# Ten parts of the output projection, one job or ten, in the table that orders TensorE's instructions

## The chip, the cores and the metric

One core of one Trainium2 chip. The metric is the device time of one execution of the kernel in microseconds (us); smaller is better. Three runs of the kernel before gave 1026.78, 1026.9 and 1029.99 us, median 1026.9.

## The reference

A trunk of four decoder layers over 512 tokens of width 1024, everything in float32. Each layer projects its input, runs attention with 16 heads of 64 value columns, multiplies the heads' outputs by a SiLU gate, projects back, adds the result to the scaled input and normalizes. The attention differs by layer: latent attention (layers 0 and 3), a sliding window of 128 with sinks (layer 1), a softmax with a forget-gate bias (layer 2).

```python
for i in range(DEPTH):                       # 4 layers
    kind = i % 3                             # mla, swa, fox, mla
    h = x @ w_in                             # q, k, v (or their low ranks) and the gate
    o = attention(h)                         # 16 heads x 64, 512 x 1024
    y = (o * jax.nn.silu(gate)) @ w_out      # the output projection: contraction over 1024
    x = layernorm(alpha * x + y) * ln_g[i] + ln_b[i]
```

## The kernel before

**Numbers in halves.** TensorE works here on fp32r values. Each operand is kept as a high part and a low rest, and each product is made of three matmuls: high by high, low by high, high by low. So a projection of one output tile of 128 tokens by 512 columns over 1024 rows takes 8 blocks of 128 rows, 3 matmuls each.

**A layer.** `run_heads` (L654) issues the middle of a layer: the projections that are still missing (K, Q, R, V and gate G, as generators that issue one matmul at a time and then yield), and for each head three kinds of attention steps. The s steps are logits: matmuls into a PSUM tile `ss` for each block of 128 queries; VectorE adds the bias or mask and finds the maximum (L885, L947, L1067, L1069), and after the last block `softmax_tail` (L445) has ScalarE make the exponentials, VectorE the reciprocal `rs`, and GpSimd and ScalarE the scaling of the P tiles. The t steps transpose P on TensorE into a PSUM tile `ptt`; `pt_evac` (L497) copies it to `PT` as high (ScalarE, L500) and low (VectorE, L325). The o steps multiply PT with V into the single PSUM tile `oo`; at the end of a head ScalarE copies one half (L543) and VectorE adds the other (L544), which frees `oo`. After the second head of a pair, the pair's output is multiplied by its gate (L551, GpSimd, or VectorE for the last pair) and becomes a block of `oT`: high by a ScalarE cast (L552), low by a subtraction (L325, on GpSimd or VectorE). Block k of `oT` is head pair k. Two blocks share one tile, so `oT` of blocks 4 and 5 has one name.

**The output projection.** An output tile is (half, tb): half 0 or 1 of the 1024 columns, tb one of four blocks of 128 tokens. `out_mm` (L570) issues its matmuls for a list of blocks ks, three per block: k's weight block `w` (or `wo`) against `oT` block k. Each output tile accumulates in a PSUM tile of its own; those of half 0, tb 0 to 2 come from the pool of three banks `pp`, which the projections use as well. `out_part` (L557) makes ten parts, in this order: (0,0), (0,1), (0,2) each over blocks 0 to 5, the same three over block 6, then (1,0), (1,1), (1,2), (0,3) over blocks 0 to 6. Block 7 comes after the attention, in `finish` (L705).

**TensorE's order.** The order of TensorE's instructions is not left to the scheduler. `ORDER` (above `layer_units`) holds one string of words for each layer; a word is a letter and a count. s, t and o take so many steps from the logits, the transposes and the P·V products of the heads in turn. f, g and h take so many steps from the first, second and third job of a list `jobs` (f = `jobs[0]`, g = `jobs[1]`, h = `jobs[2]`). A job is `[steps left, generator]`; when `jobs[0]` has no steps left it is dropped and the others move up. The projections of `STREAM` are a job each, and behind them stands one job of nominally 1000 steps, which is the whole of `out_part`. A g or h that points past the end of the list takes the last job (`min(..., len(jobs) - 1)`). So once only the output projection is left, f, g and h all mean the same: its next matmul. The last words of three layers:

```python
# layer 1: ... s2 f1 s2 f19 s2 g1 s2 g14 o3 t4 o5 f1 t3 g1 f7 o8
# layer 2: ... f6 t3 f3 g14 o1 g1 s2 t3 o3 f1 g1 s2 h6 t4 h2 s2 h1 f2 o1 f1 o3 f1 s2 t3 f3 t3 o8
# layer 3: ... f5 o4 f7 t4 f1 g4 o1 f1 s6 f6 o3 t3 f4 t3 f2 o8
```

`tail` (L692) and `finish` (L705) take what is left of the output projection from `st["order"]`, in counts of their own, around the last two heads. The other engines execute in the order that the scheduler gives them; each waits for TensorE and for each other through semaphores.

Of the kernel before, what the change touches and what calls it, by code (L numbers as in the profile page):

```python
# [200 lines left out]
class Net:  # L201
# [355 lines left out]
    def out_part(self, layer, st):  # L557

        st["acc"] = {}
        st["done"] = 0  # L560
        st["stat"] = self.p_st.tile([128, NT, 4], F32, tag="stat", name=self.nm("stat"))
        self.load_residual(layer, st)
        parts = [(0, tb, range(6)) for tb in range(3)] + [(0, tb, [6]) for tb in range(3)]
        parts += [(half, tb, range(7)) for half, tb in ((1, 0), (1, 1), (1, 2), (0, 3))]
        for half, tb, ks in parts:
            for _ in self.out_mm(layer, st, half, tb, list(ks), False):
                st["done"] += 1 if self.fine else 3
                yield

    def out_mm(self, layer, st, half, tb, ks, stop):  # L570
        if (half, tb) not in st["acc"]:
            if (half, tb) in ((1, 0), (1, 1)):
                st["acc"][(half, tb)] = self.ps_s.tile([128, 512], F32, tag="ss", name=self.nm("po"))
            elif (half, tb) in ((1, 2), (0, 3)):
                st["acc"][(half, tb)] = self.ps_t.tile([128, 512], F32, tag="pt", name=self.nm("po"))
            else:
                st["acc"][(half, tb)] = self.bank()
        out = st["acc"][(half, tb)][:]
        oT = st["oT"]
        return self.tokproj_steps(out, lambda k: (self.W(layer, "O", half, k // 2), (k % 2) * 512), 512,  # L580
                                  lambda k, a, b: oT[k // 2][:, k % 2, a, b * 128:(b + 1) * 128], tb, ks, ks[0] == 0, stop, 3)
# [72 lines left out]
    def run_heads(self, layer, st, make, pre=None, npre=0):  # L654

        kind = layer % 3
        st["P"], st["PT"], st["oT"] = {}, {}, []
        st["np"] = 3 if kind == 0 else 2
        self.heads = 0

        def size(n):
            return {"K": 6, "Q": 9, "R": 9}.get(n, 24) if kind == 0 else 96 if n == "V" else 24

        def logits():
            for h in range(H - 1):
                if h == 13 and kind == 0:
                    self.cq_done(layer)
                for i, f in enumerate(st["s_fn"](h, st)):
                    for j, _ in enumerate(f()):
                        if i == NT - 1 and j == st["np"] - 1:  # L670
                            self.head_done()
                        yield

        jobs = [[npre, pre]] if npre else []
        jobs += [[size(n), make[n](a)] for n, a in STREAM[kind]]
        st["order"] = self.out_part(layer, st)
        jobs.append([1000, st["order"]])
        runs = {"s": logits(), "t": chain.from_iterable(f() for h in range(H - 2) for f in st["t_fn"](h, st)),
                "o": chain.from_iterable(self.attn_pv(h, st) for h in range(H - 2))}
        self.fine = True  # L680
        with self.tc.manual_schedule(engines={mybir.EngineType.PE}):
            for w in ORDER[layer].split():
                for _ in range(int(w[1:])):
                    job = jobs[min("fgh".index(w[0]), len(jobs) - 1)] if w[0] in "fgh" else [0, runs[w[0]]]
                    next(job[1])
                    job[0] -= 1
                    while jobs[0][0] == 0:
                        jobs.pop(0)
            assert len(jobs) == 1 and all(next(r, None) is None for r in runs.values())
            self.tail(layer, st)  # L690

    def tail(self, layer, st):  # L692
# [448 lines left out]
```

## Time and profile before

| | before |
|---|---|
| median of three runs | 1026.9 us |
| the profiled execution's own time | 1026.01 us |
| its span, first to last instruction | 1024.2 us |
| mean granted TensorE clock | 0.986 |
| ScalarE, VectorE, GpSimd busy | 620.8, 598.3, 510.7 us |
| DMA | 116.79 MB, 114 GB/s in the mean |

Layer 1 ends near 470 us, layer 2 near 770 us. Engines are named PE (TensorE matmul), PEld (its weight load), ACT (ScalarE), DVE (VectorE), POOL (GpSimd), SP (DMA issue). A row of a timeline holds the start, the time from the first start to the last end, the engine, line, operation, tiles, form and count; in brackets the idle time before it and what ended that. Durations of neighbouring matmuls overlap, since they are pipelined: the pace is read from start to start. A row of the windows view holds the stretch, its length, PE's busy time and instructions, the granted clock, and the DMA's share and GB/s.

### The profile page before, as it was taken

Reading aid. Unit: us, or ns where it says so; the run is one execution under the profiler, and the core shown is the slowest. Engines: PE = TensorE matmul, PEld = TensorE weight load, DVE = VectorE, ACT = ScalarE, POOL = GpSimd, SP = SyncE. Lnnn points to the kernel's source line nnn. Section 1 sums busy time; section 2 is a strip of 40 time slices with the busy share of each in tenths; the row PEclk is TensorE's granted clock in tenths of the full one; section 3 lists DMA queues with packets and bytes.
Section 4 is the critical chain, followed back from the end, with each engine's and each line's share of the span. In section 5 each row is a group of like instructions: output and inputs, shape, how many; then the busy total and the mean of one; then the engine's idle time right before and its main releaser. Section 6 shows DMA issues by size and latency. Waiting matters only on the chain.

```text
span 1024.2 us, 16213 instructions
## 1 busy us (share of the span) xinstructions
PE 985.8 (96%) x5512; PEld 856.9 (84%) x5512; DVE 598.3 (58%) x1501; ACT 620.8 (61%) x1354; POOL 510.7 (50%) x572
## 2 busy tenths in 40 slices
PE   8999999999999999899999999997999999999995
PEld 7979888877988888688888888985779888888784
DVE  2467666935546667528325644664547466667827
ACT  4378888843357777523446766663533478888722
POOL 5746655335156663432556666543254647664213
PEclk9999999999999999899999999998999999999998
DMA  6353332634342213223434323353224354334322
GB/s 225 119 157 92 98 106 66 205 111 146 133 143 84 83 63 124 91 94 128 133 120 141 105 88 120 91 144 120 84 84 146 97 145 127 85 94 124 103 62 83
DMA packets 37795, 116.79 MB, mean 114 GB/s; under 512 B 5440, under 2 KB 5696, under 8 KB 37456
## 3 DMA queue, kind: packets, MB, share of 16 engines
q1 hardware_dynamic: 37712, 115.75, 36.5%
q8 instruction: 44, 0.72, 0.3%
q14 instruction: 39, 0.32, 0.1%
HBM read 92.62 MB, written 8.42 MB: 99 GB/s over the span
## 4 chain that ended last, share of the span: by engine, by line
PE 47%; DVE 3%; issue 2%; POOL 1%; ACT 1%; DMA 1%; DVEq 0%; POOLq 0%; SPq 0%; ACTq 0%
PE pp L322 31%; PE ss L322 4%; PE po L322 4%; PE oo L322 3%; PE ptt L514 3%; DMA wr<-in_w 1%; PE pxt L389 1%; POOL r L650 1%; DVE w L310 1%; DVE r L634 0%; POOL P L462 0%; DVE PT L325 0%; ACT P L451 0%; DVE wo L310 0%; DVE r L586 0%
## 5 line engine op out<-in xcount | busy, mean ns | idle before, releaser
L322 PE MATMUL pp<-xT,w 128*128 128x512 f32 (+1 forms) x1440 | 352.4, 387 | 0.0
L310 POOL TENSOR_TENSOR w<-wr,w 128x512 fp32r<-128x512 f32 (+1 forms) x202 | 242.2, 1224 | 193.0 <-ACT w L306 127.2
L322 PEld LDWEIGHTS pp<-xT,w 128*128 128x128 f32 x1440 | 256.1, 188 | 44.2
L462 POOL TENSOR_TENSOR P<-P,rs 128x256 f32<-128x256 f32 (+2 forms) x192 | 113.0, 616 | 136.8 <-DVE rs L457 131.3
L306 ACT CAST w<-wr 128x1024 fp32r<-128x1024 f32 (+5 forms) x121 | 116.1, 964 | 87.4 <-PE pp L322 43.5
L451 ACT ACTIVATE P<-P,m 128x256 f32<-128x256 f32 (+3 forms) x256 | 137.8, 539 | 45.9 <-DVE m L1069 17.0
L325 DVE TENSOR_TENSOR PT<-ptt,PT 128x384 fp32r<-128x384 f32 (+1 forms) x176 | 104.0, 600 | 52.6 <-ACT PT L500 51.3
L500 ACT CAST PT<-ptt 128x384 fp32r<-128x384 f32 (+1 forms) x176 | 88.3, 515 | 47.6 <-PE ptt L514 34.6
L322 PE MATMUL pp<-w,xT 128*128 128x256 f32 (+2 forms) x768 | 112.7, 300 | 2.9 <-ACT xT L393 2.5
L322 PEld LDWEIGHTS pp<-w,xT 128*128 128x128 f32 x768 | 105.8, 191 | 4.6 <-ACT xT L393 3.1
L322 PE MATMUL oo<-PT,v 128*128 128x256 f32 (+3 forms) x512 | 106.6, 313 | 2.3 <-DVE o L544 1.6
L322 PEld LDWEIGHTS oo<-PT,v 128*128 128x128 f32 x512 | 83.5, 189 | 14.0 <-DVE o L544 2.6
L322 PE MATMUL pp<-w,oT 128*128 128x512 f32 x288 | 82.5, 422 | 10.9 <-ACT oT L552 7.5
L322 PE MATMUL ss<-kt,q 128*128 128x128 f32 (+3 forms) x384 | 81.8, 328 | 2.2 <-ACT kt L838 1.6
L322 PE MATMUL pp<-cT,w 128*128 128x512 f32 x312 | 81.6, 397 | 0.0
L885 DVE CUSTOM_DVE_ANT_0 P<-ss,mask 128x128 f32<-128x128 f32 (+3 forms) x128 | 61.1, 484 | 32.4 <-PE ss L322 24.7
L514 PE MATMUL ptt<-ident,P 128*128 128x128 f32 x480 | 78.5, 275 | 1.5 <-DVE PT L325 0.8
L322 PEld LDWEIGHTS pp<-w,oT 128*128 128x128 f32 x288 | 56.0, 202 | 23.4 <-ACT oT L552 8.1
L322 PE MATMUL po<-wo,oT 128*128 128x512 f32 x288 | 71.5, 396 | 0.0
L322 PEld LDWEIGHTS ss<-kt,q 128*128 128x128 f32 x384 | 60.7, 189 | 8.8 <-ACT kt L838 2.2
L514 PEld LDWEIGHTS ptt<-ident,P 128*128 128x128 f32 x480 | 57.1, 140 | 11.8 <-PE ss L322 2.1
L544 DVE TENSOR_TENSOR o<-oo,o 64x512 f32<-64x512 f32 x64 | 43.9, 686 | 37.4 <-ACT o L543 36.7
(120 smaller groups left out, 1425.9 us busy)
## 6 DMA issues: line engine op xcount, KB each, us to landing
wr<-in_w SPq DMA_DIRECT2D x106, 512.0 KB, 3.5
q<-rq SPq DMA_DIRECT2D x64, 128.0 KB, 2.4
xd<-r SPq DMA_DIRECT2D x12, 512.0 KB, 2.9
r<-xd SPq DMA_DIRECT2D x12, 512.0 KB, 3.4
wr<-in_w SPq DMA_DIRECT2D x16, 336.0 KB, 3.4
kd<-kd SPq DMA_DIRECT2D x20, 256.0 KB, 3.2
tq<-in_cs SPq DMA_DIRECT2D x8, 512.0 KB, 4.0
cb<-cd SPq DMA_DIRECT2D x16, 256.0 KB, 3.9
```

Source lines behind the costliest of these rows:

```text
L306: nc.scalar.copy(w[0][:, :c], r[:, :c])
L310: eng.tensor_tensor(w[1][:, a:b], r[:, a:b], w[0][:, a:b].bitcast(F32), op=ALU.subtract)
L322: self.nc.tensor.matmul(out, l, r, start=start, stop=stop)
L325: (eng or self.nc.vector).tensor_tensor(out, src, hi.bitcast(F32), op=ALU.subtract)
L389: nc.tensor.transpose(v, xt[:, c:c + 128], self.ident[:])
L451: nc.scalar.activation(v, v, AF.Exp, bias=m[:, c:c + 1], scale=-1.0, accum_out=sums[:, c:c + 1])
L462: nc.gpsimd.tensor_tensor(v, v, rs[:, c:c + 1].to_broadcast([128, v.shape[1]]), op=ALU.mult)
L500: nc.scalar.copy(pt[:, 0, :n], ps[:, :n])
L514: nc.tensor.transpose(ps[:, c:c + 128], Ps[qb][:, kb * 128:(kb + 1) * 128], self.ident[:])
L544: nc.vector.tensor_tensor(o[a, :], o_ps[a, :], o[a, :], op=ALU.add)
L650: nc.gpsimd.tensor_tensor(v, v, st["gb"][2 * part + c][:], op=op)
L885: nc.vector.tensor_tensor_reduce(out=P[:, :n], in0=ps[:, :n], in1=self.mask[:, S - n:], scale=1.0, scalar=3e38, op0=ALU.add, op1=ALU.min, ...
```

## The change

`out_part` returns a list of ten jobs, one for each part, in place of one generator over all ten, and `run_heads` appends them to `jobs`. The clamp on g and h is gone. What is left of the jobs after the table's last word becomes `st["order"]`, chained in the old order, for `tail` and `finish`. The load of the residual is still made at the first matmul of the first part (through the test for `"r"`); the tile `stat` is now made when `out_part` is called. The table `ORDER` is the same.

```diff
@@ out_part
-        self.load_residual(layer, st)
         parts = [(0, tb, range(6)) for tb in range(3)] + [(0, tb, [6]) for tb in range(3)]
         parts += [(half, tb, range(7)) for half, tb in ((1, 0), (1, 1), (1, 2), (0, 3))]
-        for half, tb, ks in parts:
+
+        def part(half, tb, ks):
+            if "r" not in st:
+                self.load_residual(layer, st)
             for _ in self.out_mm(layer, st, half, tb, list(ks), False):
                 st["done"] += 1 if self.fine else 3
                 yield
+
+        return [[3 * len(ks), part(half, tb, ks)] for half, tb, ks in parts]
@@ run_heads
-        st["order"] = self.out_part(layer, st)
-        jobs.append([1000, st["order"]])
+        jobs += self.out_part(layer, st)
...
-                    job = jobs[min("fgh".index(w[0]), len(jobs) - 1)] if w[0] in "fgh" else [0, runs[w[0]]]
+                    job = jobs["fgh".index(w[0])] if w[0] in "fgh" else [0, runs[w[0]]]
...
-            assert len(jobs) == 1 and all(next(r, None) is None for r in runs.values())
+            assert all(next(r, None) is None for r in runs.values())
+            st["order"] = chain.from_iterable(g for _, g in jobs)
```

What moves: in layer 0 no g or h falls on the output projection, and nothing moves. In layers 1, 2 and 3 the same matmuls are issued, 19, 30 and 6 positions of the table holding another one than before; at the table's end each layer has issued the same set. GpSimd, VectorE and SP keep their order. On ScalarE one instruction moves, in layer 1: the scaling of a P tile of 256 columns (L460) stands behind one PT cast (L500) and one copy of `oo` (L543) in place of ahead of them.

TensorE in layer 1, before, from the last matmuls of block 4 of part (0,0) on (`pp_4700` is the output tile (0,0), `oT_4452` holds blocks 4 and 5, `pp_4763` is (0,1), `ss` are logits):

```order
L322 MATMUL pp_4700<-w_4591,oT_4452 128x512 x2
L322 MATMUL pp_4700<-w_4592,oT_4452 128x512
L322 MATMUL ss_4735<-kd_3240,q_4493 128x256 x2
L322 MATMUL pp_4700<-w_4591,oT_4452 128x512
L322 MATMUL ss_4741<-kd_3240,q_4493 128x256 x2
L322 MATMUL pp_4700<-w_4591,oT_4452 128x512
L322 MATMUL pp_4700<-w_4592,oT_4452 128x512
L322 MATMUL pp_4763<-w_4395,oT_3634 128x512 x2
```

The same place now (`pp_4740` is the output tile (0,1)):

```order
L322 MATMUL pp_4700<-w_4592,oT_4453 128x512 x2
L322 MATMUL pp_4700<-w_4593,oT_4453 128x512
L322 MATMUL ss_4735<-kd_3240,q_4494 128x256 x2
L322 MATMUL pp_4740<-w_4396,oT_3635 128x512
L322 MATMUL ss_4742<-kd_3240,q_4494 128x256 x2
L322 MATMUL pp_4740<-w_4396,oT_3635 128x512
L322 MATMUL pp_4740<-w_4397,oT_3635 128x512
L322 MATMUL pp_4740<-w_4396,oT_3635 128x512 x2
```

Block 5 of (0,0), which stood between and behind the two logit pairs, has given its place to (0,1) over blocks 0 to 4; its three matmuls come back after the next P·V steps and transposes, mixed with block 5 of (0,1).

TensorE in layer 2, before, from block 4 of part (0,0) on (`pp_7572` is (0,0), `oT_7294` holds blocks 4 and 5, `pp_7651` is (0,1), `oo` is P·V of head 12):

```order
L322 MATMUL pp_7572<-w_7496,oT_7294 128x512 x2
L322 MATMUL pp_7572<-w_7497,oT_7294 128x512
L322 MATMUL pp_7572<-w_7496,oT_7294 128x512 x2
L322 MATMUL pp_7572<-w_7497,oT_7294 128x512
L322 MATMUL pp_7651<-w_7350,oT_6167 128x512 x2
L322 MATMUL pp_7651<-w_7351,oT_6167 128x512
L322 MATMUL pp_7651<-w_7350,oT_6167 128x512 x2
L322 MATMUL pp_7651<-w_7351,oT_6167 128x512
L322 MATMUL pp_7651<-w_7416,oT_6720 128x512 x2
L322 MATMUL pp_7651<-w_7417,oT_6720 128x512
L322 MATMUL pp_7651<-w_7416,oT_6720 128x512 x2
L322 MATMUL oo_7663<-PT_7617,v_7075 128x512
```

Layer 2 now, where block 5 of (0,0) comes back (`pp_7572` is (0,0), `pp_7648` is (0,1), `pp_7692` is (0,2)); ahead of these rows stand block 4 of (0,0) and 12 matmuls of (0,1):

```order
L322 MATMUL pp_7648<-w_7497,oT_7295 128x512 x2
L322 MATMUL oo_7663<-PT_7617,v_7076 128x512
L322 MATMUL pp_7648<-w_7498,oT_7295 128x512
L322 MATMUL ss_7669<-kd_7409,q_7346 128x128 x2
L514 MATMUL ptt_7674<-ident,P_7435 128x128
L514 MATMUL ptt_7674<-ident,P_7447 128x128 x2
L322 MATMUL oo_7663<-PT_7617,v_7076 128x512
L322 MATMUL oo_7663<-PT_7636,v_7076 128x384 x2
L322 MATMUL pp_7572<-w_7497,oT_7295 128x512
L322 MATMUL pp_7648<-w_7497,oT_7295 128x512
L322 MATMUL ss_7686<-kd_7409,q_7346 128x256 x2
L322 MATMUL pp_7692<-w_7351,oT_6168 128x512 x2
```

The first matmul on block 5 (`pp_7572`) now follows 15 matmuls of (0,1), a P·V group, a logit pair and three transposes in place of following block 4 directly; its second and third come after nine matmuls of (0,2).

## The prediction

> **What bounds the kernel now.** The page comes first: TensorE (PE) is busy for 96% of the span, and no other engine for more than 61%. So time is to be won only where PE waits or where its clock is held down. The clock's row shows that in three slices out of 40 (the first digit is the start): two of them show an 8.
>
> ```profile
> PE 985.8 (96%) x5512; PEld 856.9 (84%) x5512; DVE 598.3 (58%) x1501; ACT 620.8 (61%) x1354; POOL 510.7 (50%) x572
> PEclk9999999999999999899999999998999999999998
> ```
>
> Next the waits of PE, summed by the line that waited and by what ended the wait. The largest are matmuls of the output projection (`pp`) that wait for `oT`:
>
> ```profile
> PE pp L322 <- ACT oT L552: 7.5, 2, 3.9
> PE pp L322 <- POOL oT L325: 3.2, 2, 2.6
> ```
>
> PE's timeline around them shows two places, the first in layer 1. Fifteen matmuls (part (0,0), blocks 0 to 4) take 407.01 to 410.42; then PE stands 3.60 us, until the high half of block 5 is there. Behind the stall 14 matmuls take 415.76 to 421.55. The last row is the o8 of the table, head 13.
>
> ```profile
> 407.01 3.56 PE L322 MATMUL pp<-w,oT 128*128 128x512 f32 x15
> 410.42 0.40 PE L322 MATMUL ss<-kd,q 128*128 128x256 f32 x2
> 414.41 0.80 PE L322 MATMUL pp<-w,oT 128*128 128x512 f32 x1 [3.60 <-ACT oT L552]
> 415.00 0.63 PE L322 MATMUL ss<-kd,q 128*128 128x256 f32 x2
> 415.76 5.96 PE L322 MATMUL pp<-w,oT 128*128 128x512 f32 x14
> 421.55 0.52 PE L322 MATMUL oo<-PT,v 128*128 128x256 f32 x3
> ...
> 425.33 1.05 PE L322 MATMUL oo<-PT,v 128*128 128x256 f32 x8
> ```
>
> The second place is in layer 2: one matmul of block 5 after 3.90 us, the next after 2.63 us more, since its low half comes later still.
>
> ```profile
> 700.40 0.95 PE L322 MATMUL pp<-w,oT 128*128 128x512 f32 x3
> 705.24 0.80 PE L322 MATMUL pp<-w,oT 128*128 128x512 f32 x1 [3.90 <-ACT oT L552]
> 708.67 5.91 PE L322 MATMUL pp<-w,oT 128*128 128x512 f32 x13 [2.63 <-POOL oT L325]
> 714.39 0.53 PE L322 MATMUL oo<-PT,v 128*128 128x512 f32 x1
> ...
> 716.08 0.63 PE L322 MATMUL pp<-w,oT 128*128 128x512 f32 x2
> ...
> 724.25 0.56 PE L322 MATMUL oo<-PT,v 128*128 128x256 f32 x3 [0.20 <-DVE PT L325]
> ```
>
> Last the windows of 1 us at the edges of the slow stretches. The column behind the count is the granted clock:
>
> ```profile
> 414.00:415.00 1.00, 0.59 (x1) 0.65 0.12 46
> 421.00:422.00 1.00, 1.00 (x7) 0.93 0.00 0
> 704.00:705.00 1.00, 0.00 (x0) 0.72 0.51 187
> 714.00:715.00 1.00, 1.00 (x5) 0.66 0.00 0
> ```
>
> If the clock is 1 or 0.5, a mean of 0.65 puts 0.70 us of that window at half, so the drop is at 414.30; likewise the rise is at 421.14, and the second pair of edges lies at 704.44 and 714.68. A stall here costs twice: the wait, and the matmuls behind it at half pace, for 6.84 us and 10.24 us of slow clock. 10.24 is 1.5 times 6.84, so 3.42 us looks like the unit. The Trainium skill ("TensorE: Matmul & The Clock Gate", Part 1, "What's actually happening") has the array's clock halved after one idle window of 4096 cycles, 3413 ns, on a free-running count; two and three such windows are 6.83 and 10.24, so this trace agrees.
>
> **The change part by part.** The pace of a part's matmul at full clock is (410.42 − 407.01)/15 = 0.227 us.
>
> *Layer 1, what goes.* In place of block 5 the table's g1 and g14 now take (0,1) over blocks 0 to 4. Its `oT` blocks and weights are those that (0,0) has just used, and with three banks in `pp` it takes over that of gate 6, two projections back; were that bank still being read, the wait would at most be today's. The 3.60 us go. At half clock the single matmul took 0.59 for 0.23 (414.41 to 415.00), the logit pair 0.76 for about 0.40 (415.00 to 415.76 against the row at 410.42), the 14 took 5.79 for 3.18: 0.36 + 0.36 + 2.61 = 3.3 us go as well. So PE would reach o8 not at 425.33 but at 425.33 − 6.9 = 418.4.
>
> *Layer 1, what is late next.* Block 5 itself comes after o3, t4 and o5, past 415.6, and its high half is there at 413.74 + 0.62 = 414.36, its low half one subtraction later. But o8 needs `oo`, which is free once head 12 has been copied, and ScalarE does that behind the exponentials of head 14:
>
> ```profile
> 414.04 0.42 DVE L947 CUSTOM_DVE_ANT_0 P<-ss,ali 128x256 f32<-128x256 f32 x1
> 415.67 0.42 DVE L947 CUSTOM_DVE_ANT_0 P<-ss,ali 128x256 f32<-128x256 f32 x1 [1.20 <-PE ss L322]
> 424.38 0.54 DVE L325 TENSOR_TENSOR PT<-ptt,PT 128x384 fp32r<-128x384 f32 x1
> ...
> 413.74 0.62 ACT L552 CAST oT<-o 128x512 fp32r<-128x512 f32 x1 [0.20 <-POOL o L551]
> 416.40 0.41 ACT L451 ACTIVATE P<-P,m 128x128 f32<-128x128 f32 x1 [2.05 <-DVE m L449]
> 418.28 0.28 ACT L454 ACTIVATE es<-m,sink 128x4 f32<-128x4 f32 x1
> 419.06 0.51 ACT L460 ACTIVATE P<-P,rs 128x256 f32<-128x256 f32 x1 [0.50 <-DVE rs L457]
> 422.54 0.59 ACT L500 CAST PT<-ptt 128x512 fp32r<-128x512 f32 x1 [2.97 <-PE ptt L969]
> 423.15 0.58 ACT L543 COPY o<-oo 64x512 f32<-64x512 f32 x1
> 423.77 0.68 DVE L544 TENSOR_TENSOR o<-oo,o 64x512 f32<-64x512 f32 x1
> ```
>
> The last bias step of head 14 (415.67) waited 1.20 for PE; it now follows its neighbour at once, so the exponentials run from 415.2 to 417.4 (416.40 and 418.56 less 1.2). Then PT 0.59, copy 0.58, VectorE 0.68: `oo` is free at 419.2, 0.8 after PE asks. The second PT tile comes after the L460 that has moved (0.51), its own cast (about 0.5) and the subtraction (0.54): 418.5 + 1.55 = 420.1, some 0.5 more after two products. New wait 1.3 us. Net: 6.9 − 1.3 = **5.6 us**.
>
> *Layer 2, what goes.* Between 701.35 (end of the row at 700.40) and 714.39 PE issues 14 matmuls, which at 0.227 are 3.18 us: 13.04 − 3.18 = 9.9 us, of which 3.90 and 2.63 are the two waits and the rest is the slow clock. All 14 now read blocks that are there.
>
> *Layer 2, what is late next.* Block 5 of (0,0) comes after 15 matmuls (3.4 us) and a group of P·V, logits and transposes, about 1.5 us (714.39 to 716.08, less one matmul): at 701.35 + 4.9 = 706.2. Its next pass, the low half, follows eleven more matmuls (2.5) and about 1 us of attention: 709.7.
>
> ```profile
> 704.59 0.60 ACT L552 CAST oT<-o 128x512 fp32r<-128x512 f32 x1
> 707.36 1.26 POOL L325 TENSOR_TENSOR oT<-o,oT 128x512 fp32r<-128x512 f32 x1
> 720.97 0.58 ACT L543 COPY o<-oo 64x512 f32<-64x512 f32 x1 [1.57 <-PE oo L322]
> ```
>
> Neither row waited for PE: high is there at 705.2, low at 708.6, both 1 us early. The copies behind do wait for PE (720.97) and move with it. At the end of the group stands today's 0.20 us for a PT tile; with ScalarE and VectorE less far ahead I add 0.3. Net: 9.9 − 0.3 = **9.6 us**.
>
> *Layer 3 and the rest.* Layer 3 exchanges six positions. The two rows of waits for `oT` hold four waits, 3.60, 3.90, 2.63 and about 0.6, so at most 0.6 can be its; and block 5 moves there by three or four matmuls: 0, with bounds of −0.6 and +0.2. The order of GpSimd, VectorE and SP is unchanged, so no DMA moves past another; residual loads and weights are released by PE's steps and follow them. The moved L460 is counted above. The early `stat` tile costs no instruction.
>
> *Sum.* 5.6 + 9.6 = 15.2 us off the profiled execution's 1026.01: 1010.8. The median lies 0.9 above that execution, so on the median **1011.7 us**.
>
> **The rivals.**
>
> *The slow clock is a matter of phase.* The drop at 414.30 falls 0.1 us before PE restarts; a little later and layer 1 would have kept full clock. If the timed runs of before had no such stretch, only 15.2 − 3.3 = 11.9 go: 1015.0. The Trainium skill's free-running window ("TensorE: Matmul & The Clock Gate", Part 1, as above) stands behind this rival: by it a stall of 3.60 holds a whole window only in few phases. Against it: the profiled execution is the fastest time shown, not a slow one. Also, a much shorter stall at the end of layer 2 has a slow stretch too:
>
> ```profile
> 765.09 0.66 PE L389 MATMUL pxt<-ident,r 128*128 128x128 f32 x4 [2.03 <-DVE r L634]
> 766.00:767.00 1.00, 0.98 (x5) 0.50 0.80 97
> ```
>
> One window of 3.42 at half is 1.7 us, which may go there or come at another layer's end.
>
> *Layer 2's wait moves to o8.* If the softmax of head 14 does not come forward, PE stands before head 13's product as long as it stands now, and only layer 1's 5.6 go: 1021.3. For it: the chain of ScalarE and VectorE is long. Against it: the copy at 720.97 and the step at 415.67 waited for PE.
>
> *Nothing is left of it.* Both layers are bound by that chain and the waits only change their name: 1026.9.
>
> *Slower.* The place is o8 of layers 1 and 2, the price the same waits as today, but now ending just before the long product groups of the tail, so that each gives one more window at half clock, 1.7 each: 1026.9 + 3.4 = 1030.3. It decides once ScalarE's copy of head 12 comes later than today's 423.15 and 720.97. Nothing in the rows holds it back so far.
>
> *The change does nothing.* The order of the instructions shows that it does; no chance.
>
> **How the numbers follow.** Forecast 0.72; phase 0.12; layer 2's wait moves 0.10; nothing left 0.03; slower 0.03. Range: downwards, 1.7 for the stretch at 766 and 1.5 for the new waits, 1008.5; upwards, the 3.3 of layer 1, 1.7 for one more stretch and 1.5 for waits that I have not seen, 1018.2. That holds the first two cases, 0.84, and little of the third. A measurement of this kernel tells about 0.3%, 3 us, from no change. So faster 0.94, same 0.03, slower 0.03.
>
> **What would show it right or wrong.** Right: no row of PE waiting for `oT` above 1 us; clock 1.00 where it was 0.5 near 415 and 710; a new row of `oo` waiting for `o` or PT, about 1 us, in layer 1; mean clock up from 0.986 by about 0.008 (17 us of slow stretch, half of it lost). Wrong: a wait above 3 us at o8, or slow windows elsewhere in layers 1 and 2; then the step that failed is "what is late next".

## The result, and the profile after

The changed kernel takes 1015.03 us in the median of four runs (1013.75 to 1017.59), the kernel before 1026.84 in the runs beside them (1026.27 to 1029.99): a ratio of 0.9882, 95% interval 0.9854 to 0.991. Two further comparisons of the same two kernels, below, give 0.9876 both times. So the change takes off 1.2%, 12 to 14 us. The forecast was 1011.7 us, range 1008.5 to 1018.2.

| | before | after |
|---|---|---|
| median | 1026.84 us | 1015.03 us |
| the profiled execution's own time | 1026.01 us | 1013.75 us |
| its span | 1024.2 us | 1012.0 us |
| mean granted TensorE clock | 0.986 | 0.994 |

The page of after, TensorE's busy time and the row of its clock: the two slices with an 8 inside the span are gone, and PE has 6.5 us less of busy time for the same 5512 matmuls, since fewer of them ran at half pace.

```profile
PE 979.3 (97%) x5512; PEld 853.5 (84%) x5512; DVE 601.6 (59%) x1501; ACT 620.8 (61%) x1354; POOL 511.0 (50%) x572
PEclk9999999999999999999999999999999999999998
```

PE's waits in after, summed by line and releaser (us in total, times, longest us): no row of `pp` waiting for `oT` is left among them. At the top stands P·V waiting for `oo` instead.

```profile
PE oo L322 <- DVE o L544: 5.6, 4, 2.2
PE pxt L389 <- DVE r L638: 4.3, 5, 1.9
PE pc L810 <- DVE cqk L783: 2.1, 1, 2.1
```

Of the 5.6 us only 1.75 are the new wait in layer 1. 2.16 stand in layer 0, where nothing moved, and 1.37 in layer 3, where before has 0.95.

PE's timeline of after in layer 1. The first row is part (0,0) over blocks 0 to 4; 14 matmuls of (0,1) now run in 3.37 us straight behind the logits, where PE stood 3.60 us and then took 5.96 for 14. The next row shows where the price is paid: at o8 PE waits 1.75 and then 0.17 for head 13.

```profile
410.65 3.56 PE L322 MATMUL pp<-w,oT 128*128 128x512 f32 x15
414.05 0.40 PE L322 MATMUL ss<-kd,q 128*128 128x256 f32 x2
414.29 0.40 PE L322 MATMUL pp<-w,oT 128*128 128x512 f32 x1
...
414.76 3.37 PE L322 MATMUL pp<-w,oT 128*128 128x512 f32 x14
...
423.67 0.62 PE L322 MATMUL oo<-PT,v 128*128 128x256 f32 x3 [1.75 <-DVE o L544]
424.45 0.80 PE L322 MATMUL oo<-PT,v 128*128 128x256 f32 x5 [0.17 <-DVE PT L325]
...
430.70 4.33 PE L322 MATMUL pp<-w,oT 128*128 128x512 f32 x18
434.87 2.94 PE L322 MATMUL po<-wo,oT 128*128 128x512 f32 x12
```

The same in layer 2: 17 matmuls (three of block 4, 14 of (0,1)) without a gap, block 5 at 704.98 and, its low half, within the three at 708.34. The only wait left is the 0.21 for a PT tile at o8 that stood there before.

```profile
699.46 4.13 PE L322 MATMUL pp<-w,oT 128*128 128x512 f32 x17
703.43 0.39 PE L322 MATMUL oo<-PT,v 128*128 128x512 f32 x1
...
704.98 0.63 PE L322 MATMUL pp<-w,oT 128*128 128x512 f32 x2
...
708.34 0.86 PE L322 MATMUL pp<-w,oT 128*128 128x512 f32 x3
...
713.15 0.56 PE L322 MATMUL oo<-PT,v 128*128 128x256 f32 x3 [0.21 <-DVE PT L325]
```

Windows of 1 us of after (stretch, length, PE's busy time and count, granted clock, DMA share, GB/s). Where the clock was at half in before, it is at 1.00; behind the new wait, one stretch at half clock has come.

```profile
414.00:415.00 1.00, 1.00 (x8) 1.00 0.58 85
425.00:426.00 1.00, 1.00 (x9) 0.73 0.00 0
428.00:429.00 1.00, 1.00 (x5) 0.57 0.00 0
704.00:705.00 1.00, 1.00 (x10) 1.00 0.01 2
```

Its edges, read as in the prediction: the mean of 0.73 puts 0.54 us of that window at half, so the drop is at 425.46; 0.57 puts 0.86 there, so the rise is at 428.86; 3.40 us, one unit.

So that stages can be compared wherever they start, this table takes start-to-start distances on PE from each profile: in layers 1 and 2 from the first matmul of part (0,0) to the first of `po` (the tile (1,0)); and the time from (0,0) of layer 1 to (0,0) of layer 2. The last column has the stretches at half clock behind the start of the program and ahead of its end.

| kernel | (0,0) of layer 1 starts | layer 1 | layer 2 | layer 1 to 2 | at half clock |
|---|---|---|---|---|---|
| before | 407.01 | 28.80 | 36.27 | 289.05 | 6.84 in layer 1, 10.24 in layer 2, 3.41 ahead of layer 3 |
| after | 410.65 | 24.22 | 26.13 | 284.47 | 3.41 in layer 1 |
| after, second profile | 410.99 | 23.91 | 26.12 | 284.38 | 3.41 ahead of layer 3 |
| after, third profile | 407.06 | 23.94 | 26.12 | 284.28 | none |

Layer 1 gave 4.6 us (4.9 in the other two profiles) and layer 2 10.1. The profiled executions differ by only 12.26 us, since in that of after (0,0) of layer 1 starts 3.64 us later; the third profile of the same kernel starts it at 407.06, so this is no part of the change. Set against it are the 1.7 us of before's stretch ahead of layer 3.

### The profile page after: what moved, and what is told of

Its sections match the earlier page's. It is cut to its first block, busy times and chain, and to the rows that moved or that the text cites. A ratio compares the mean times of both kernels' runs of the same rounds, so it can differ in the third digit from the quotient of the medians.

```text
span 1012.0 us, 16216 instructions
## 1 busy us (share of the span) xinstructions
PE 979.3 (97%) x5512; PEld 853.5 (84%) x5512; DVE 601.6 (59%) x1501; ACT 620.8 (61%) x1354; POOL 511.0 (50%) x572
## 4 chain that ended last, share of the span: by engine, by line
PE 47%; DVE 2%; issue 2%; ACT 1%; POOL 1%; DMA 0%; DVEq 0%; POOLq 0%; SPq 0%; ACTq 0%
PE pp L322 32%; PE ss L322 4%; PE po L322 4%; PE oo L322 4%; PE ptt L514 3%; POOL r L654 1%; PE pxt L389 1%; DVE r L638 0%; DMA q<-rq 0%; DVE PT L325 0%; ACT PT L500 0%; DVE wo L310 0%; DVE r L590 0%; PE pc L810 0%; ACT wo L306 0%
## 5 line engine op out<-in xcount | busy, mean ns | idle before, releaser
L500 ACT CAST PT<-ptt 128x384 fp32r<-128x384 f32 (+1 forms) x176 | 88.4, 515 | 35.4 <-PE ptt L514 24.4
L322 PE MATMUL pp<-w,oT 128*128 128x512 f32 x288 | 76.1, 398 | 0.0
L514 PEld LDWEIGHTS ptt<-ident,P 128*128 128x128 f32 x480 | 57.1, 140 | 11.8 <-PE ss L322 2.1
L322 PEld LDWEIGHTS pp<-cT,w 128*128 128x128 f32 x312 | 56.6, 188 | 10.4
```

The lines of the kernel that those rows point to most:

```text
L322: self.nc.tensor.matmul(out, l, r, start=start, stop=stop)
L500: nc.scalar.copy(pt[:, 0, :n], ps[:, :n])
L514: nc.tensor.transpose(ps[:, c:c + 128], Ps[qb][:, kb * 128:(kb + 1) * 128], self.ident[:])
```

## The experiments

The theory: PE's two stalls for block 5 are filled with matmuls that were ready, and the half-clock stretches behind them go with them; a smaller wait for `oo` takes their place in layer 1. The rivals: the gain is mostly clock (then warming the array alone brings it), or one layer carries all of it, or filling is enough wherever block 5 then stands.

**The change itself again.** No edit; run with the next three kernels, on one chip.

> The changed kernel once more, unaltered. In the two traces part (0,0) of layer 1 begins at 407.01 us before and at 410.65 after, although no instruction ahead of it has moved. If that is chance (a DMA that lands late, VectorE kept waiting by GpSimd), the new trace begins it anywhere between about 406 and 411 and the median lies near 1015. If the change itself costs something ahead of its place, it begins at 410.5 or later again. Under both, from there to the first matmul of (1,0) in layer 1 it takes 22.5 to 24.3 us (28.8 before), and from the end of block 4 in layer 2 on as in the trace of after.

Measured: 1014.38 us (1013.42 to 1015.05) against 1027.33, ratio 0.9876 (0.9858 to 0.9894). A third time, beside the last three kernels of this section:

> The changed kernel a third time, beside the others: 1014.4 to 1015.0 again. The start of (0,0) in layer 1 lies between 407 and 412 if it is chance, at 410.6 to 411.0 if it belongs to the change. From there to (0,0) of layer 2 284.1 to 284.5, in layer 2 26.1 to the first matmul of (1,0).

Measured: 1013.91 us (1010.31 to 1016.89) against 1027.54, ratio 0.9876 (0.985 to 0.9902). The stage times are in the table above. The wait at o8 of layer 1 comes in all profiles of this order: 1.75, 1.60 and 1.63 for `oo`, and 0.17 more.

**Ten jobs in layer 2 alone.** Elsewhere the parts are one job with the clamp, as before.

```diff
-        jobs += self.out_part(layer, st)
+        parts = self.out_part(layer, st)
+        split = layer in (2,)
+        jobs += parts if split else [[1000, chain.from_iterable(g for _, g in parts)]]
...
-                    job = jobs["fgh".index(w[0])] if w[0] in "fgh" else [0, runs[w[0]]]
+                    i = "fgh".index(w[0]) if w[0] in "fgh" else 0
+                    i = i if split else min(i, len(jobs) - 1)
+                    job = jobs[i] if w[0] in "fgh" else [0, runs[w[0]]]
```

> Ten jobs in layer 2 alone; layers 1 and 3 keep one job. If the gain is the stalls for oT and the half clock behind them, layer 2 gives 9.9 to 10.1 us: 1026.8 - 10 = 1016.8, the stall of 3.6 us in layer 1 stays. If the time depended on the three layers together (phase of the clock window, the start of later layers), it would be off that by more than 3 us.

Measured: 1017.31 us (1015.15 to 1021.18), ratio 0.9906 (0.9871 to 0.9941). Layer 2 takes 26.11 in place of 36.27, layer 1 keeps its stall:

```profile
419.27 0.50 PE L322 MATMUL pp<-w,oT 128*128 128x512 f32 x1 [3.63 <-ACT oT L552]
...
420.63 5.05 PE L322 MATMUL pp<-w,oT 128*128 128x512 f32 x14 [0.62 <-POOL oT L325]
```

Here the 14 matmuls behind the stall take 5.05 where before's took 5.96, and the wait for the low half shows, 0.62: the stall is the same, but only one unit at half clock followed it, not two, and it begins later, behind the 419.27 matmul, which ran at full pace.

**Ten jobs in layer 1 alone.** The same edit with `split = layer in (1,)`.

> Ten jobs in layer 1 alone. Stalls and half clock: 28.80 - 24.22 = 4.6 us with a slow window behind head 13's product, 6.3 us without: 1020.5 to 1022.2. The two waits for oT in layer 2 (3.90 and 2.63) stay. Rival, that layer 1's gain is eaten by its new wait for oo and the slow window: 1026.

Measured: 1022.38 us (1018.11 to 1027.45), ratio 0.9948 (0.9923 to 0.9974), 0.2 us above the range expected. Layer 1 takes 23.78, with 1.51 and 0.17 of waits at o8 and no stretch at half clock behind them; layer 2 keeps both its waits and three units at half clock:

```profile
422.35 0.62 PE L322 MATMUL oo<-PT,v 128*128 128x256 f32 x3 [1.51 <-DVE o L544]
423.13 0.79 PE L322 MATMUL oo<-PT,v 128*128 128x256 f32 x5 [0.17 <-DVE PT L325]
...
428.31 2.51 PE L322 MATMUL pp<-w,oT 128*128 128x512 f32 x10
431.42 2.11 PE L322 MATMUL pp<-w,oT 128*128 128x512 f32 x8 [0.60 <-POOL oT L325]
433.36 2.94 PE L322 MATMUL po<-wo,oT 128*128 128x512 f32 x12
...
702.62 0.79 PE L322 MATMUL pp<-w,oT 128*128 128x512 f32 x1 [3.62 <-ACT oT L552]
706.05 5.72 PE L322 MATMUL pp<-w,oT 128*128 128x512 f32 x13 [2.64 <-POOL oT L325]
```

The two halves give 10.0 and 5.0 us (1027.33 less 1017.31 and less 1022.38), together 15.0 against 13.0 for the whole, which is within their intervals. So the layers are worth about what the prediction gave them (9.6 and 5.6), and nothing here shows that one hides the other.

**The clock without the order.** The kernel before, with matmuls put ahead of block 5 whose product is overwritten: 14 in layers 1 and 2, and 11 more ahead of the low half in layer 2. They keep the array busy through the stall and do none of the work.

```diff
@@ out_part of before
-            for _ in self.out_mm(layer, st, half, tb, list(ks), False):
+            for n, _ in enumerate(self.out_mm(layer, st, half, tb, list(ks), False)):
...
+                if self.fine and (half, tb) == (0, 0) and len(ks) == 6:
+                    self.fill(layer, st, {15: 14, 16: 11 if layer == 2 else 0}.get(n + 1, 0) if layer in (1, 2) else 0)
+    def fill(self, layer, st, n):
...
+            for _ in range(n):
+                self.mm(st["acc"][(0, 1)][:], st["oT"][0][:, 0, 0, 128:256], w[0][:, :512], True, True)
```

> The kernel before, with extra matmuls that keep TensorE busy while it would stand for oT: 14 into the bank of (0,1) ahead of the first matmul of block 5 in layers 1 and 2, and 11 more ahead of its second in layer 2. Their product is overwritten when (0,1) begins. The waits for oT are as long as before, only filled. If the half clock comes from TensorE standing still, both slow stretches go and with them 3.3 + 3.3 us: 1020.2. If the matmuls behind the stall are slow for another reason (other engines, memory), the time stays at 1026.8; if the fill itself costs, it is above.

Measured: 1025.52 us (1022.84 to 1028.63), ratio 0.9984 (0.9968 to 1.0001). In its profile no stretch at half clock is left in the two places: the 14 matmuls behind layer 1's stall take 3.47 us, not 5.96, and the block's matmuls still wait after the filling ones. Two other stretches stand elsewhere in this profile, 6.84 us in layer 0 and 3.42 us ahead of layer 3.

```profile
417.82 0.50 PE L322 MATMUL pp<-w,oT 128*128 128x512 f32 x1 [0.47 <-ACT oT L552]
...
419.17 3.47 PE L322 MATMUL pp<-w,oT 128*128 128x512 f32 x14 [0.62 <-POOL oT L325]
...
706.84 3.06 PE L322 MATMUL pp<-w,oT 128*128 128x512 f32 x12 [1.15 <-ACT oT L552]
710.34 3.25 PE L322 MATMUL pp<-w,oT 128*128 128x512 f32 x13 [0.43 <-POOL oT L325]
```

Layer 1 takes 26.42 and layer 2 34.02, so the clock was worth 2.38 and 2.25 us, 4.6 together, of the profiled execution, and the order is worth the rest: 26.42 − 23.91 = 2.5 and 34.02 − 26.12 = 7.9. The median, however, fell by 1.8 us only (0 to 3.3 by the interval), so it lies nearer to the number expected if the clock were worth nothing. That the gain is mostly clock is refuted. Why the clock's share is smaller in the medians than in the profile is taken up below.

**Filling is not enough if block 5 comes back early.** The changed kernel, with the words of layer 2's table that follow g14 so put that all three matmuls of block 5 of (0,0) stand directly behind the 14 of (0,1); the later words name the jobs as they then move up.

```diff
- ... f3 g14 o1 g1 s2 t3 o3 f1 g1 s2 h6 t4 h2 s2 h1 f2 o1 f1 o3 f1 s2 ...
+ ... f3 g14 f3 o1 f1 s2 t3 o3 f1 s2 g6 t4 g2 s2 g1 o1 f1 o3 f1 s2 ...
```

> The changed kernel, but in layer 2 all three matmuls of block 5 of (0,0) come back at once behind the 14 of (0,1), in place of one after the next products and two after nine of (0,2). If each pass waits for its own half of oT, the first waits 0.7 us and the second until the subtraction on GpSimd ends, 3.3 us more: 30.1 us from the first output projection matmul of layer 2 to the first of (1,0) there for 26.1, more with a slow window behind it; the median 4 to 5.7 us above the changed kernel's. If the 14 matmuls ahead are the whole of the gain and where block 5 returns does not matter, 26.1 and no change.

Measured: 1017.32 us (1016.64 to 1018.33), ratio 0.991 (0.9886 to 0.9935), 3.4 us above the changed kernel on the same chip, less than the 4 to 5.7 expected. The 14 matmuls cover 3.2 us of the stall, not the low half:

```profile
701.43 0.49 PE L322 MATMUL pp<-w,oT 128*128 128x512 f32 x1 [0.87 <-ACT oT L552]
704.88 0.94 PE L322 MATMUL pp<-w,oT 128*128 128x512 f32 x2 [2.95 <-POOL oT L325]
```

Layer 2 takes 32.0: 3.82 us of waits and a unit at half clock (1.7) over the changed kernel's 26.1 make 31.6. So in this profile filling alone brings 4.3 of layer 2's 10.1 us (36.27 less 32.0); the rest is the late return of block 5, of its low half above all.

**Filling the new wait.** In the changed kernel o8 of layer 1 waits while matmuls of the output projection are ready. One edit puts nine more of them ahead of it; the second, with it, also moves part (1,0) over blocks 0 to 6 ahead of block 6 of the half-0 tiles, so that more parts come before block 6. First the one alone:

```diff
- (layer 1) ... o3 t4 o5 f1 t3 g1 f7 o8
+ (layer 1) ... o3 t4 o5 f1 t3 g1 f16 o8
```

> The same nine matmuls ahead of head 13's product, but block 6 stays where it is. The wait for oo goes; block 6 is then reached some 1.8 us earlier, while its oT comes at the same time or 0.3 later: a wait of about 2.5 us there, nothing gained, 284.3 to 284.6 us from (0,0) of layer 1 to that of layer 2, the median as the changed kernel's. If block 6 were not bound by its oT, 282.5 us.

Measured: 1015.39 us (1013.21 to 1016.33), ratio 0.9888 (0.9862 to 0.9914): no gain on the changed kernel. The wait at o8 is gone, and block 6 is now reached before its low half is there; at the last row the eight matmuls also run at half clock.

```profile
429.30 0.50 PE L322 MATMUL pp<-w,oT 128*128 128x512 f32 x1 [0.33 <-ACT oT L552]
431.89 3.78 PE L322 MATMUL pp<-w,oT 128*128 128x512 f32 x8 [2.09 <-POOL oT L325]
```

From (0,0) of layer 1 to that of layer 2 it takes 286.73 us, 2.4 more than the third profile of the changed kernel: behind these waits 6.84 us at half clock have come, which the expectation did not have.

Then both:

```diff
@@ out_part, beside the edit of the table
         parts += [(half, tb, range(7)) for half, tb in ((1, 0), (1, 1), (1, 2), (0, 3))]
+        if layer == 1:
+            parts.insert(3, parts.pop(6))
```

> The changed kernel with the new wait of layer 1 filled: nine more matmuls of (0,2) ahead of head 13's product (f16 for f7), and behind it (1,0) over blocks 0 to 6 ahead of block 6 of the tiles of half 0. If the wait for oo is only a matter of what stands ahead of it, both it (1.5 to 1.75 us) and the 0.6 us for block 6 go: from the start of (0,0) in layer 1 to that of layer 2 281.9 us for 284.3, the median 2.4 below the changed kernel's. If (1,0) finds its weights not split yet, the wait comes back there and the time is the same or longer.

Measured: 1008.8 us (1008.11 to 1009.18), ratio 0.9826 (0.9802 to 0.985); the changed kernel has 1013.91 on the same chip. PE's timeline of layer 1: 17 matmuls ahead of o8, no wait at o8, and 21 of `po` ahead of the nine of block 6, which do not wait either.

```profile
416.58 4.15 PE L322 MATMUL pp<-w,oT 128*128 128x512 f32 x17
420.57 1.31 PE L322 MATMUL oo<-PT,v 128*128 128x256 f32 x8
...
426.25 5.04 PE L322 MATMUL po<-wo,oT 128*128 128x512 f32 x21
431.13 2.21 PE L322 MATMUL pp<-w,oT 128*128 128x512 f32 x9
```

From (0,0) of layer 1 to that of layer 2 it takes 281.08 us against 284.28 of the third profile of the changed kernel: 3.2 us, of which 1.8 are the wait at o8 and 0.6 that for block 6; the other 0.8 were not traced to a place. The medians lie 5.1 apart, the two profiled executions only 1.5 (1010.31 and 1008.8), so what the medians have beyond this stage can't be placed either. This version beats both kernels.

## Why the prediction was right, and where it was off

*Layer 1, what goes.* Right. The 3.60 us and the half-clock stretch are gone, and the stage lost 4.6 to 5.0 us in four profiles (28.80 against 24.22, 23.91, 23.94 and 23.78). The split was not quite as the prediction had it: of its 3.3 us of slow clock only 2.4 can be had by the clock alone, since half-pace matmuls covered the wait for block 5's low half, 0.6, which shows once they are fast. In the sum both go, so the sum held.

*Layer 1, what is late next.* The place was right, the term mis-sized: 1.3 us forecast for `oo` and PT, 1.68 to 1.92 measured in four profiles (1.51 + 0.17 to 1.75 + 0.17). The chain of after shows the step. VectorE's instruction L449, which takes the minimum of the maxima and the sink's value, stands ahead of head 14's exponentials; having moved forward, it now falls on GpSimd's subtraction for `oT`. VectorE of after, then its GpSimd:

```profile
418.71 0.92 DVE L449 TENSOR_SCALAR m<-m,nsink 128x4 f32<-128x4 f32 x1
...
422.93 0.68 DVE L544 TENSOR_TENSOR o<-oo,o 64x512 f32<-64x512 f32 x1
```

```profile
418.32 1.28 POOL L325 TENSOR_TENSOR oT<-o,oT 128x512 fp32r<-128x512 f32 x1 [0.73 <-ACT oT L552]
```

And before, where GpSimd was done when VectorE came to it:

```profile
416.13 0.23 DVE L449 TENSOR_SCALAR m<-m,nsink 128x4 f32<-128x4 f32 x1
```

```profile
414.43 1.27 POOL L325 TENSOR_TENSOR oT<-o,oT 128x512 fp32r<-128x512 f32 x1 [0.73 <-ACT oT L552]
```

0.92 for 0.23, ending at 419.63 where GpSimd ends at 419.60: 0.7 us, and the chain behind it comes later by as much: `oo` was free at 423.61, against the forecast's 419.2, which with this profile's 3.64 us of later start is 422.84. The prediction moved L449 forward and kept its duration. It is 0.92 in all three profiles of the changed kernel.

That such a row depends on GpSimd could be read from before. L449 stands 16 times in its profile. Eight rows take 0.23 us, and GpSimd does nothing beside them; eight take 0.56 to 1.31, and each of these begins while GpSimd is at work. The longest, with the GpSimd row beside it, ends at 311.38 where GpSimd ends at 311.35:

```profile
310.07 1.31 DVE L449 TENSOR_SCALAR m<-m,nsink 128x4 f32<-128x4 f32 x1
308.82 2.53 POOL L310 TENSOR_TENSOR w<-wr,w 128x512 fp32r<-128x512 f32 x2
```

In none of the ten profiles does L449 take more than 0.23 us without GpSimd at work beside it. The Trainium skill ("SBUF — State Buffer", "SBUF: two separate sides") describes a port pair that VectorE, in some forms of instruction, and GpSimd share and hold for a whole instruction, so that the later one is blocked; the common end agrees. No run here shows in which form L449 is.

*A half-clock stretch at o8.* The prediction had one only in the slower rival. It came in one profile of three of the unaltered changed kernel and in that with the early return, whose layer 1 is the same, and cost little. From the second P·V row of o8 to the matmuls ahead of `po` after takes 6.25 us (424.45 to 430.70), the kernel with layer 1 alone, without the stretch, 5.18 (423.13 to 428.31): 1.1 more. From there to `po` it is 4.17 against 5.05, since block 6 is then there when PE comes to it and the 0.60 for its low half is gone: 0.9 come back.

*Layer 2.* Right on both sides. The stage lost 10.14 us against 9.9 worked out; the 0.3 us added for the PT tile did not come (0.21 for 0.20). High and low half of block 5 were forecast ready 1 us ahead of PE. ScalarE and GpSimd of after:

```profile
703.53 0.60 ACT L552 CAST oT<-o 128x512 fp32r<-128x512 f32 x1
```

```profile
706.37 1.29 POOL L325 TENSOR_TENSOR oT<-o,oT 128x512 fp32r<-128x512 f32 x1
```

Ready at 704.13 and 707.66; used at 704.98 and, the low half, by the second of the three matmuls at 708.34, near 708.6: 0.9 us early each. The kernel with the early return shows what lies on the other side of this margin.

*Layer 3 and the rest.* Near enough: from (0,0) of layer 3 to its first `po` takes 27.40 us before, 27.81, 27.21 and 27.73 after. That is 0.4 and 0.3 longer and 0.2 shorter, against a forecast of 0 and an upper bound of 0.2.

*The sum and the median.* 15.2 us were forecast; the stages gave 14.7 (4.58 + 10.14) in the first pair of profiles, but the medians 11.8, 13.0 and 13.6. The term that was too large on the medians is, as far as the runs show, the clock. The prediction took the profiled execution of before for a typical one. Each run lists its mean clock: 30 timed runs of before lie between 0.982 and 0.992, 0.9875 in the mean, so the profiled one, at 0.986, had more slow clock than two in three of them. 14 runs of the changed kernel lie between 0.987 and 0.995, 0.9924 in the mean, where its profile had 0.994. The time lost to the clock is (1 − clock) x span: 14.3 and 6.1 us in the two profiles, 8.2 apart, as the prediction's 0.008 had it; in the timed runs 12.8 and 7.7, 5.1 apart. The 3.1 us between these are the size of what is missing, if all of it lay on the path. That it did is not shown: a straight line through the 30 runs of before gives only 0.5 us of time for each us so lost. One run of the kernel with ten jobs in layer 1 alone even has a mean clock of 0.94 at 1021.1 us, below that kernel's median. The kernel with the filling matmuls points the same way: 4.6 us of clock in the profile, 1.8 in the median.

The prediction's argument against a price so small was that the profiled execution is the fastest time shown. It was ahead for another reason as well: (0,0) of layer 1 starts at 407.01 there, the earliest of all ten profiles. (The prediction also reads two 8s in the clock's row. There are three; the third, in the last slice, stands in after too.)

So the rival of the phase, 1015.0, holds in part: the forecast's mechanism is the one that acts, but its price for the clock was that of one execution. The rival also says that with another phase layer 1 would have kept full clock. In the kernel with ten jobs in layer 2 alone it did not: its stall of 3.63 us brought one unit at half clock in place of two. That the measured median is the rival's 1015.0 to a tenth is chance. In which stage a timed run has its stretches isn't recorded, and stays open.

*The other rivals.* The wait of layer 2 did not move to o8 (0.21). That nothing is left falls with the single layers, 0.9906 and 0.9948. The slower rival had its place right, o8 of layer 1, but the wait is half of the one removed, and in layer 2 there is none.

## What to carry to other kernels

When the busiest engine waits for one operand, give it work whose operands are there, and let what waits come back only behind the last part of that operand; filling alone brought less than half of layer 2's gain. Then look at what stands next in the same order, since each edit here moved a wait to the next operand (`oo`, then block 6) until both were filled together. Price a clock stretch by many timed runs, not by the one execution that has a profile; and when an instruction is moved, look at what runs on the other engines at its new place before its old duration is used.

## What the runs showed of the hardware

*The unit of the half clock, and what starts it.* All stretches at half clock in the layers are multiples of one unit, 3.41 us (3.41, 6.84, 10.24), as the prediction read. Within one execution their edges lie whole numbers of units apart, on one grid: in before the drops at 414.30, 704.44 and 765.88 are 290.14 and 61.44 us apart, 85.0 and 18.0 units.

New is how little idle time starts one: in after, a stall of 1.75 us and one of 0.17 behind it, at o8. In the unit ahead of the drop at 425.46, from 422.05 on, PE stood for 1.6 us and then, but for those 0.17, worked up to the drop. By the Trainium skill ("TensorE: Matmul & The Clock Gate", Part 1, "What's actually happening") the drop follows an idle window; here the window was not wholly idle.

Stalls of 1.60 and 1.63 us at the same place started none in the other two profiles, but one of 1.63 did in the kernel with the early return. So the stall's length does not decide; what the five profiles with this stall differ in is its place on the grid. One window each of the early return and of the second and third profile of the changed kernel gives the grid:

```profile
421.00:422.00 1.00, 0.83 (x8) 0.96 0.00 0
754.00:755.00 1.00, 0.73 (x4) 0.66 0.00 0
9.00:10.00 1.00, 1.00 (x8) 0.68 1.04 422
```

In the early return the drop is at 421.92, and the unit ahead of it holds the whole stall (418.99 to 420.62) and the 0.17; in after, too, nearly all of it lies in one unit, 1.8 us idle in each. In the second profile the drop at 754.32 lies 97 units behind 423.26, an edge within the stall (422.25 to 423.85); in the third the one at 9.36 lies 120 units ahead of 418.9, within the stall again (418.31 to 419.94), and with layer 1 alone an edge at 421.25 parts the stall from 420.84 to 422.35. In these three no unit holds more than 1.3 us of idle time, and no stretch follows. That the place decides fits all five, but where the limit lies, and whether idle time alone is what counts, stays open: of the wait of 2.16 us near 210 in after, 1.8 lie in one unit on the same grid, and they started none.

*An operation of VectorE can take several times as long beside GpSimd.* L449 takes 0.23 us alone and up to 1.31 beside GpSimd. In layer 0, with no instruction moved, the scaling of `cqk` took 2.54 us in two profiles of the changed kernel and 0.55 in the third and in before. VectorE of after's profile, and of the third:

```profile
47.71 2.54 DVE L783 TENSOR_SCALAR cqk<-cqk,rr 128x384 f32<-128x384 f32 x1 [3.34 <-POOL rr L782]
```

```profile
47.85 0.55 DVE L783 TENSOR_SCALAR cqk<-cqk,rr 128x384 f32<-128x384 f32 x1 [3.27 <-POOL rr L782]
```

In the first, VectorE ends 0.2 us after a run of GpSimd operations that began at 47.65 and ended at 50.03; PE's wait of 2.1 us for `cqk` in the table of waits is the price. In both profiles GpSimd starts 0.06 us ahead of VectorE, so its coming first is not what decides between 2.54 and 0.55; what does was not tried and stays open.

*Layer 0 scatters.* Part (0,0) of layer 1 starts between 407.0 and 411.9 us in the profiles of kernels whose layer 0 is the same. The row above is one cause; another, in after, is a wait of 2.16 us for `oo` near 210, where before has 0.38. With a scatter of this size, a difference of 3 us between two profiles needs the stages set side by side before it is put down to an edit.
